# SSM groups of a two-block network on one core: the gate product in a PSUM bank of its own, and five scalings moved from VectorE to ScalarE

## The chip, the core and the metric

The kernel runs on one core of one Trainium2 chip. The metric is device time in microseconds of one execution. The engines that matter are TensorE (PE in the rows; PEld is its weight load), VectorE (DVE), ScalarE (ACT), GpSimd (POOL) and SyncE (SP, which issues nearly all the loads). Each works through its own queue in order, and waits for the others on semaphores.

## What is computed

Two network blocks follow each other, each of two layers, on a sequence of 256 rows of 1024 columns in float32. The change lies in the second layer of the second block, in its state-space (SSM) mixer. Cut to that, the reference is:

```
z, xbc, dt = split(u @ w_in)                      # u: 256 x 1024
xs, B, C   = split(silu(conv3(xbc) + bias))       # 8 groups of 4 heads of 64, state 128
dt         = softplus(dt + dt_bias)               # forward and backward
y_f, _ = ssd_chunked(xs, dt[fwd], A[0], B, C, h0_fwd)      # chunks of 128
y_b, _ = ssd_chunked(flip(xs), flip(dt[bwd]), A[1], flip(B), flip(C), h0_bwd)
y = y_f + flip(y_b) + D_skip * xs
y = rmsnorm_per_group(y * silu(z)) * norm_g       # 8 groups of 256 columns
out = y @ w_out
```

and inside a chunk of `ssd_chunked`, for each head: a diagonal part (C B^T times a decay matrix, times dt x), a part from the state at the chunk's start, and the state handed to the next chunk, `h1 = decay * h0 + (decayed B)^T x`.

## The kernel before, in words

Float32 products are made of three products in the chip's replicated float32: every operand is split in a high part (a rounded copy) and a low part (the rest). For weights `Weights` (line 50 on) does this as they arrive: ScalarE casts the high half `wh` (L57), VectorE subtracts to get the low half `wl` (L58), in parts of 512 columns; each of the two has five buffers. `mm3` and `up` (L181) multiply hi by hi, hi by lo, lo by hi.

The SSM mixer (`ssm`, line 1742 on) works through eight groups. For each, `proj` makes four tiles of x, B and C (`xbc`: 24 matmuls each into `ps_xbc`, then a convolution by ScalarE and VectorE, L1548 to L1554) and the gate `z` (48 matmuls in two halves of 24, one for each 128 rows, into `ps_z`), whose silu is `z_sz` (tanh on ScalarE, L1737, and a product on VectorE, L1738). A group needs twelve parts of weights: eight for the four tiles, four for the gate.

`group(g)` (line 1798 on) takes the projections of group g:
- transposes of x, B (`ps_xt`, `ps_bt`) and the product C B^T (`ps_cb`); ScalarE copies x (`z_xt`), B (`z_Bt`) and C B^T (`z_CB`); VectorE makes the weighted x (`z_xw`, L1666) and starts y with the skip, `y = D * x` (L1666, `z_y<-ps_xt`);
- the state of the second chunk: product `ps_h` (L1833), decay of the old one on VectorE (L1666, `z_h<-z_h,z_ediag`), their sum (L1836);
- the decay matrices G: outer sums in PSUM (`ps_r`, L1841, L1842), sixteen exponentials of 128 columns on ScalarE (L1846), the two directions added and multiplied by CB (L1848, L1849), one half of the rows on VectorE, the other on GpSimd;
- for each 128 rows: the part from the states (`ps_off`, scaled by VectorE, L1666, summed by GpSimd, L1858 and L1859) and the diagonal part (`ps_yd`, L1863, added by VectorE, L1864);
- y times the gate on GpSimd (L1865), squares with a sum on ScalarE (`yj`, L1869), an inverse root by eleven small instructions on VectorE (L268 to L273), the norm scaling on VectorE (L1873);
- later, in the middle of the next group, `ends`: y is transposed (`ps_t`, L300), scaled by norm_g on VectorE (`evac_T`, L322), and split in `z_yh` and `yl` (L259, L260).

Group g runs beside the projections of group g + 1; generators put their instructions between the matmuls, and the framework's scheduler sets the order on each queue by priority. PSUM has eight banks: `ps` two (projection tiles and gate in turn), `pa` three (`ps_xt`, `ps_r`, `ps_off`, `ps_yd`, the transposes of y), `pl` two (`ps_bt`, `ps_cb`), `pd` one (`ps_h` in this stage). Since the gate takes its turn in `ps`, the second projection tile after it needs the bank that the gate fills.

Of the kernel before, what the change touches and what calls it, by code (L numbers as in the profile page):

```python
# [8 lines left out]
F32 = mybir.dt.float32  # L9
F32R = mybir.dt.float32r  # L10
I32 = mybir.dt.int32
AF = mybir.ActivationFunctionType
ALU = mybir.AluOpType

P = 128
S = 256
# [48 lines left out]
class Core:  # L65
# [225 lines left out]
    def evac_T(self, src, gcol, bcol, dst, ps=None):  # L291

        nc = self.nc
        hi, lo = dst
        n = src.shape[2] // P
        if n == 8:
            self.spare = self.SPARE
        def trans(pt, t, j):
            for c in range(2):
                nc.tensor.transpose(pt[:, c, t], src[:, t, (j + c) * P:(j + c + 1) * P], self.ident)  # L300
        if ps is None:
            pts = [(self.ps, self.pl)[j // 2 % 2]([P, 2, 2, P], "ps_t") for j in range(0, n, 2)]
            for t in range(2):
                for j in range(0, n, 2):
                    trans(pts[j // 2], t, j)
        for j in range(0, n, 2):
            if ps is None:
                ptj = pts[j // 2]
            else:
                ptj = ps([P, 2, 2, P], "ps_t")  # L310
                for t in range(2):
                    trans(ptj, t, j)

            val = self.t2([P, 2, S], name="ev_t")
            for c in range(2):
                g = gcol[:, j + c:j + c + 1]
                b = 0.0 if bcol is None else bcol[:, j + c:j + c + 1]
                pt = ptj[:, c].rearrange("p t i -> p (t i)")
                if self.EV[j // 2 % 4]:
                    nc.scalar.activation(val[:, c], pt, AF.Identity, bias=b, scale=g)  # L320
                elif bcol is None:
                    nc.vector.tensor_scalar(val[:, c], pt, g, None, op0=ALU.mult)  # L322
                else:
                    nc.vector.tensor_scalar(val[:, c], pt, g, b, op0=ALU.mult, op1=ALU.add)  # L324
            self.split(hi[:, j:j + 2], lo[:, j:j + 2], val)
# [798 lines left out]
class Second(Core):  # L1124
# [600 lines left out]
    def proj(self, g, xp):  # L1725

        nc = self.nc
        w = self.io["ssm_w_in_2"][0]
        tiles = self.xbc(g, (2 * g, 2 * g + 1, 16 + g, 24 + g), xp)
        pz = self.ps([P, 2, S], "ps_z2")  # L1730
        wz = [self.wsplit(w[k * P:(k + 4) * P, g * S:(g + 1) * S].rearrange("(k p) n -> p k n", p=P), 4, S) for k in (0, 4)]
        for t in range(2):
            for k in range(8):
                self.mm3(pz[:, t], tuple(q[:, k, t * P:(t + 1) * P] for q in xp), wz[k // 4].at(k % 4), k == 0, k == 7)
            self.tick()
        sz = self.w2("sz", [P, 2, S], bufs=3)
        nc.scalar.activation(sz, pz, AF.Tanh, scale=0.5)  # L1737
        nc.vector.scalar_tensor_tensor(sz, sz, 1.0, pz, op0=ALU.add, op1=ALU.mult)  # L1738
        return tiles, sz

    def ssm(self, xp):
# [4 lines left out]
        v_, s_, g_ = nc.vector, nc.scalar, nc.gpsimd  # L1746
# [3 lines left out]
        identr = self.w2("identr", [P, P], F32R)  # L1750
        s_.copy(identr, self.ident)
        ng = self.const("normg", [P, 16], self.pool2)
        sel32 = self.const("sel", [P, 64], self.pool2)
        sel = self.w2("selr", [P, 64], F32R)
        s_.copy(sel, sel32)
        Dr = self.w2("Dr", [P, 32])
# [20 lines left out]
        wdiag, ediag = (self.w2(n, [P, 2, 32]) for n in ("wdiag", "ediag"))  # L1777
# [20 lines left out]
        def group(g, proj):  # L1798
            h0 = self.w2("h0", [P, 2, S], bufs=2)
            nc.sync.dma_start(h0.rearrange("p d n -> p (d n)"), self.h0d[g])  # L1800
            (xa, xb, Bc, Cc), sz = proj

            px = self.pa([P, 2, S], "ps_xt")
            for t in range(2):
                for c, src in enumerate((xa, xb)):
                    te.transpose(px[:, t, c * P:(c + 1) * P], src[:, t * P:(t + 1) * P], self.ident)
            xt = self.w2("xt", [P, 2, S], bufs=2)
            y = self.w2("y", [P, 2, S], bufs=2)
            xw = self.w2("xw", [P, 2, S])
            both = lambda z, t: z[:, t].rearrange("p (d r) -> p d r", d=2)[:, :, 4 * g:4 * g + 4]  # L1810
            s_.copy(xt, px)
            self.scale_heads(xw, px, wdiag[:, :, 4 * g:4 * g + 4])
            self.scale_heads(y, px, Dr[:, 4 * g:4 * g + 4])
            pb = self.pl([P, 2, P], "ps_bt")
            for t in range(2):
                te.transpose(pb[:, t], Bc[:, t * P:(t + 1) * P], self.ident)
            Bt = self.w2("Bt", [P, 2, P], bufs=2)
            s_.copy(Bt, pb)
            pcb = self.pl([P, 2, P], "ps_cb")
            for t in range(2):  # L1820
                mm(pcb[:, t], Bc[:, t * P:(t + 1) * P], Cc[:, t * P:(t + 1) * P], start=True, stop=True)
            CB = self.w2("CB", [P, 2, P], bufs=2)
            s_.copy(CB, pcb)
            yield

            G = self.w2("G", [P, 2, 2, 4, P])
            for d in range(2):
                if d:
                    yield

                    ph1 = self.psum.tile([P, 2, S], F32, tag="pd", name="ps_h1", bufs=1)
                    for e in range(2):
                        mm(ph1[:, e], Bt[:, e], xw[:, e], start=True, stop=True)  # L1833
                    h1 = self.w2("h1", [P, 2, S], bufs=2)
                    self.scale_heads(h1, h0, ediag[:, :, 4 * g:4 * g + 4])
                    v_.tensor_tensor(h1, h1, ph1, op=ALU.add)  # L1836
                for hp in range(2):
                    pr = self.pa([P, 2, S], "ps_r")
                    for e in range(2):
                        r = d * 32 + 4 * g + 2 * hp + e  # L1840
                        mm(pr[:, e], sel[:, r:r + 1].to_broadcast([P, P]), cumr, start=(e == 0), stop=False, skip_group_check=True)  # L1841
                    mm(pr, identr, trir[:, d].unsqueeze(1).to_broadcast([P, 4, P]), start=False, stop=True, skip_group_check=True)  # L1842
                    for e in range(2):
                        r = d * 32 + 4 * g + 2 * hp + e
                        for t in range(2):
                            s_.activation(G[:, d, t, 2 * hp + e], pr[:, e, t * P:(t + 1) * P], AF.Exp, bias=ncum[:, t, r:r + 1])  # L1846
            for t, z in enumerate((v_, g_)):
                z.tensor_tensor(G[:, 0, t], G[:, 0, t], G[:, 1, t], op=ALU.add)  # L1848
                z.tensor_tensor(G[:, 0, t], G[:, 0, t], CB[:, t].unsqueeze(1).to_broadcast([P, 4, P]), op=ALU.mult)  # L1849
            for t in range(2):  # L1850
                if t == 0:
                    yield
                po = self.pa([P, 2, S], "ps_off")
                for d in range(2):
                    mm(po[:, d], Cc[:, t * P:(t + 1) * P], (h0 if d == t else h1)[:, d], start=True, stop=True)
                tmp = self.t2([P, 2, S], name="yoff")
                self.scale_heads(tmp, po, both(ecum, t))
                g_.tensor_tensor(tmp[:, 0], tmp[:, 0], tmp[:, 1], op=ALU.add)  # L1858
                g_.tensor_tensor(y[:, t], y[:, t], tmp[:, 0], op=ALU.add)  # L1859
                yield  # L1860
                py = self.pa([P, 4, 64], "ps_yd")
                for h in range(4):
                    mm(py[:, h], G[:, 0, t, h], xt[:, t, h * 64:(h + 1) * 64], start=True, stop=True)  # L1863
                v_.tensor_tensor(y[:, t], py.rearrange("p h i -> p (h i)"), y[:, t], op=ALU.add)  # L1864
            g_.tensor_tensor(y, y, sz, op=ALU.mult)  # L1865
            ss = self.sm(2, "y_ss")
            junk = self.t2([P, 2, S], name="yj")
            for t in range(2):
                s_.activation(junk[:, t], y[:, t], AF.Square, accum_out=ss[:, t:t + 1])  # L1869
            v_.tensor_scalar(ss, ss, 1.0 / (4 * S), 1e-6, op0=ALU.mult, op1=ALU.add)  # L1870
            rs = self.rsqrt(ss, 2)
            for t in range(2):
                v_.tensor_scalar(y[:, t], y[:, t], rs[:, t:t + 1], 0.5, op0=ALU.mult, op1=ALU.mult)  # L1873
            ends.append(lambda: self.evac_T(y, ng[:, 2 * g:2 * g + 2], None, yp(2 * g, 2, slice(None)), self.pa))

        projs, ends = [first], []
# [253 lines left out]
```

## Time and profile before

| what | value |
|---|---|
| median of 3 runs | 2434.46 us (2431.4 to 2436.79) |
| the profiled execution's own time | 2440.55 us |
| its span in the profile | 2438.8 us |
| granted TensorE clock over the span | 0.987 |
| TensorE busy | 2327.1 us (95%) |
| VectorE busy | 1779.1 us (73%) |
| ScalarE busy | 1242.1 us (51%) |
| GpSimd busy | 174.7 us (7%) |

The span runs from the first to the last instruction that the profile shows; the execution's own time holds what lies around it. Busy shares are means over stages of different kinds. In a row of the order of time, the figure in brackets is the idle time of that engine just before the row, with what ended it. Matmuls overlap, so a row of 0.28 us may stand 0.12 us behind the one before it. The SSM groups lie from about 1981 to 2194 us.

### The profile page before, as it was taken

The page shows a single profiled execution, that of the slowest core. Times are in us where ns is not written, and L with a number is a line of the kernel's source. Part 1 is how long each engine was busy: PE and PEld are TensorE (multiplying, and loading weights), DVE is VectorE, ACT ScalarE, POOL GpSimd, SP SyncE. Part 2 cuts the span into 40 slices and gives each one's busy share as a digit, 9 for nine tenths or more (in the row PEclk, how much of TensorE's full clock was granted, in tenths as well). Part 3 has the DMA queues.
Part 4 walks back from the last instruction along what each step waited for, and adds up shares of the span by engine and source line. Part 5 has one row for each costly group of instructions (what it writes and reads, how often), then busy time and mean ns, then how long its engine had stood idle before and what let it go on. Part 6 is the DMA issues. An engine that isn't in the chain of part 4 may idle for free.

```text
span 2438.8 us, 49693 instructions
## 1 busy us (share of the span) xinstructions
PE 2327.1 (95%) x19210; PEld 2048.2 (84%) x19210; DVE 1779.1 (73%) x4082; ACT 1242.1 (51%) x2621; POOL 174.7 (7%) x230
## 2 busy tenths in 40 slices
PE   8899999999999999989999999999999999989998
PEld 6787777799998887778888898888899899877997
DVE  6768976676668868767877655887766789986666
ACT  3334435555555344344455555566555566654554
POOL 0210110000000200200000000000000012330000
PEclk9999999999999999999999999999999999999999
DMA  8645555555667654465556566523566644437664
GB/s 243 204 142 153 169 150 116 139 175 168 185 189 216 178 165 129 140 192 164 158 166 170 148 185 206 143 70 96 173 187 183 177 132 129 121 109 225 197 183 130
DMA packets 511277, 396.56 MB, mean 163 GB/s; under 512 B 49776, under 2 KB 444832, under 8 KB 510784
## 3 DMA queue, kind: packets, MB, share of 16 engines
q1 hardware_dynamic: 510096, 391.11, 54.8%
q8 instruction: 151, 2.47, 0.4%
q0 software_dynamic: 944, 2.26, 0.3%
q14 instruction: 86, 0.70, 0.1%
HBM read 386.90 MB, written 6.42 MB: 161 GB/s over the span
## 4 chain that ended last, share of the span: by engine, by line
PE 61%; issue 20%; DVE 11%; ACT 4%; DMA 3%; POOL 1%; SPq 0%; ACTq 0%; DVEq 0%; POOLq 0%
PE ps_fg L181 13%; PE ps_acc L181 9%; PE acc L181 5%; PE ps_gl L181 4%; PE ps_up L181 3%; PE ps_z L181 3%; PE ps_xbc L181 3%; DVE wl L58 2%; PE ps_br L181 2%; PE ps_qk L181 2%; PE ps_o L1487 2%; PE ps_ada L1167 1%; PE ps_q L181 1%; PE ps_pt L1479 1%; PE ps_v L181 1%
## 5 line engine op out<-in xcount | busy, mean ns | idle before, releaser
L58 DVE TENSOR_TENSOR wl<-wr,wh 128x512 fp32r<-128x512 f32 (+1 forms) x1212 | 835.5, 697 | 442.7 <-ACT wh L57 434.6
L57 ACT CAST wh<-wr 128x512 fp32r<-128x512 f32 (+1 forms) x1212 | 741.8, 620 | 796.8 <-PE ps_acc L181 158.1
L181 PE MATMUL ps_fg<-xh,wh 128*128 128x256 f32 x672 | 190.2, 283 | 1.1 <-DVE ev_t L324 1.1
L181 PE MATMUL ps_fg<-xl,wh 128*128 128x256 f32 x672 | 190.2, 283 | 0.0
L181 PE MATMUL ps_fg<-xh,wl 128*128 128x256 f32 x672 | 190.2, 283 | 0.0
L181 PE MATMUL ps_acc<-wh,hh 128*128 128x512 f32 x432 | 170.5, 395 | 0.0
L181 PE MATMUL ps_acc<-wl,hh 128*128 128x512 f32 x432 | 170.4, 394 | 0.0
L181 PE MATMUL ps_acc<-wh,hl 128*128 128x512 f32 x432 | 170.2, 394 | 0.0
L181 PE MATMUL ps_up<-xh,wl 128*128 128x256 f32 x480 | 136.0, 283 | 0.0
L181 PE MATMUL ps_up<-xl,wh 128*128 128x256 f32 x480 | 136.0, 283 | 0.0
L181 PE MATMUL ps_up<-xh,wh 128*128 128x256 f32 x480 | 135.9, 283 | 0.0
L181 PEld LDWEIGHTS ps_fg<-xh,wh 128*128 128x128 f32 x672 | 129.0, 192 | 1.7 <-ACT wh L57 1.2
L181 PEld LDWEIGHTS ps_fg<-xl,wh 128*128 128x128 f32 x672 | 129.0, 192 | 0.4
L181 PEld LDWEIGHTS ps_fg<-xh,wl 128*128 128x128 f32 x672 | 129.0, 192 | 0.0
L181 PE MATMUL ps_fg<-ch,wh 128*128 128x256 f32 x352 | 101.8, 289 | 0.0
L181 PE MATMUL ps_gl<-xh,wh 128*128 128x256 f32 x336 | 98.9, 294 | 1.9 <-ACT th L975 1.5
L181 PE MATMUL ps_fg<-ch,wl 128*128 128x256 f32 x352 | 100.6, 286 | 0.0
L181 PE MATMUL ps_fg<-cl,wh 128*128 128x256 f32 x352 | 100.0, 284 | 0.0
L181 PE MATMUL ps_gl<-xl,wh 128*128 128x256 f32 x336 | 98.5, 293 | 0.0
L181 PEld LDWEIGHTS ps_acc<-wh,hl 128*128 128x128 f32 x432 | 81.3, 188 | 19.1 <-DVE hl L260 0.2
L181 PEld LDWEIGHTS ps_acc<-wh,hh 128*128 128x128 f32 x432 | 81.5, 189 | 17.9 <-ACT hh L259 0.3
L181 PE MATMUL ps_gl<-xh,wl 128*128 128x256 f32 x336 | 96.2, 286 | 0.0
(661 smaller groups left out, 6460.8 us busy)
## 6 DMA issues: line engine op xcount, KB each, us to landing
wr<-in_w_in_dram SPq DMA_DIRECT2D x110, 512.0 KB
adw<-in_ada_w_dram SPq DMA_DIRECT2D x96, 512.0 KB
wr<-in_ssm_w_in_dram SPq DMA_DIRECT2D x72, 512.0 KB
wr<-in_ffn_w_gate_dram SPq DMA_DIRECT2D x66, 512.0 KB
wr<-in_ffn_w_up_dram SPq DMA_DIRECT2D x66, 512.0 KB
wr<-in_ffn_w_down_dram SPq DMA_DIRECT2D x66, 512.0 KB
wr<-in_w_up_dram SPq DMA_DIRECT2D x64, 512.0 KB
wr<-in_w_down_dram SPq DMA_DIRECT2D x64, 512.0 KB
```

The source lines that it names most:

```text
L57: nc.scalar.copy(hi, raw[:, i:i + self.n])
L58: nc.vector.tensor_tensor(lo, raw[:, i:i + self.n], hi.bitcast(F32), op=ALU.subtract)
L181: mm = lambda *z, **k: self.nc.tensor.matmul(*z, skip_group_check=opened, **k)
L1167: nc.tensor.matmul(pm[32 * g:32 * g + 32], self.csc[:, k], w[:, g * 256:(g + 1) * 256], start=(k == 0), stop=(k == 7))
L1479: nc.tensor.transpose(pt[:, kb], sc[e][c][:, kb * P:(kb + 1) * P], self.ident)
L1487: mm(po[HS[e], c, t], kvs[kb // 2][1][:, kb % 2, g * 64:(g + 1) * 64], ats[e][:, kb], start=(kb == 0), stop=(kb == nk - 1))
```

## The change

It does six things. The gate's product `ps_z` goes into the bank `pd`, and the state product `ps_h` takes turns in `pl` instead. Five scalings of a group move from VectorE to ScalarE: the skip (one instruction of 512 columns becomes four of 2 x 64, one for each head), the decay of the state (one of 512 becomes eight of 64), the two norm scalings (two of 256), and the two evacuations of y^T with norm_g (two of 256, where `evac_T` has two column blocks). The factor 0.5 that the norm scaling carried is put into norm_g once, by GpSimd.

```diff
@@ evac_T
-                if self.EV[j // 2 % 4]:
+                if n == 2 or self.EV[j // 2 % 4]:
                     nc.scalar.activation(val[:, c], pt, AF.Identity, bias=b, scale=g)
@@ proj
-        pz = self.ps([P, 2, S], "ps_z2")
+        pz = self.psum.tile([P, 2, S], F32, tag="pd", name="ps_z2", bufs=1)
@@ ssm
         ng = self.const("normg", [P, 16], self.pool2)
+        g_.tensor_scalar(ng, ng, 0.5, 1.0, op0=ALU.mult, op1=ALU.mult)
...
-            self.scale_heads(y, px, Dr[:, 4 * g:4 * g + 4])
+            hd = [slice(h * 64, (h + 1) * 64) for h in range(4)]
+            for h in range(4):
+                s_.activation(y[:, :, hd[h]], px[:, :, hd[h]], AF.Copy, scale=Dr[:, 4 * g + h:4 * g + h + 1])
...
-                    ph1 = self.psum.tile([P, 2, S], F32, tag="pd", name="ps_h1", bufs=1)
+                    ph1 = self.pl([P, 2, S], "ps_h1")
...
-                    self.scale_heads(h1, h0, ediag[:, :, 4 * g:4 * g + 4])
+                    for e in range(2):
+                        for h in range(4):
+                            s_.activation(h1[:, e, hd[h]], h0[:, e, hd[h]], AF.Copy, scale=ediag[:, e, 4 * g + h:4 * g + h + 1])
...
-                v_.tensor_scalar(y[:, t], y[:, t], rs[:, t:t + 1], 0.5, op0=ALU.mult, op1=ALU.mult)
+                s_.activation(y[:, t], y[:, t], AF.Copy, scale=rs[:, t:t + 1])
```

The scheduler sets the order of each queue anew. Three places show it, all in groups 4 and 5; line numbers behind the skip are 7 higher in the changed kernel (G's exponentials L1846 are L1853 there, the norm L1873 is L1880, its product with CB L1849 is L1856; the skip is L1818 and the decay L1842).

ScalarE in group 4, from the gate's tanh (`z_sz`) on, before:

```order
L1737 ACTIVATE z_sz<-ps_z_25983 128x512
L57 CAST wh<-wr 128x512 x3
L1548 COPY xp_23988<-ps_xbc 128x256
L1549 ACTIVATE z_xbc<-ps_xbc,c_convw 128x256
L1811 COPY z_xt<-ps_xt 128x512
L1818 COPY z_Bt<-ps_bt 128x256
L1823 COPY z_CB<-ps_cb 128x256
L57 CAST wh<-wr 128x512 x2
L1548 COPY xp_23989<-ps_xbc 128x256
```

ScalarE at the same place, now:

```order
L1738 ACTIVATE z_sz<-ps_z_26024 128x512
L57 CAST wh<-wr 128x512 x2
L1842 ACTIVATE z_h_26626<-z_h_26502,z_ediag 128x64 x3
L57 CAST wh<-wr 128x512
L1548 COPY xp_23988<-ps_xbc 128x256
L1549 ACTIVATE z_xbc<-ps_xbc,c_convw 128x256
L1813 COPY z_xt<-ps_xt 128x512
L1823 COPY z_Bt<-ps_bt 128x256
L1828 COPY z_CB<-ps_cb 128x256
L1818 ACTIVATE z_y<-ps_xt,z_Dr 128x2x64
L1880 ACTIVATE z_y<-z_y,rs_y 128x256 x2
L1818 ACTIVATE z_y<-ps_xt,z_Dr 128x2x64 x3
```

Three decays, four skips and two norm scalings came in ahead of G's exponentials, and the two casts behind `z_CB` left this place.

ScalarE in group 5, from the copy of x to the first exponentials (`z_G`), before:

```order
L1811 COPY z_xt<-ps_xt 128x512
L1818 COPY z_Bt<-ps_bt 128x256
L1823 COPY z_CB<-ps_cb 128x256
L1869 ACTIVATE yj,y_ss<-z_y 128x256 x2
L57 CAST wh<-wr 128x512 x2
L1548 COPY xp_23989<-ps_xbc 128x256
L1549 ACTIVATE z_xbc<-ps_xbc,c_convw 128x256
L1846 ACTIVATE z_G<-ps_r,z_ncum 128x128 x8
```

ScalarE at the same place, now:

```order
L1813 COPY z_xt<-ps_xt 128x512
L1823 COPY z_Bt<-ps_bt 128x256
L1876 ACTIVATE yj,y_ss<-z_y 128x256 x2
L1818 ACTIVATE z_y<-ps_xt,z_Dr 128x2x64 x4
L1828 COPY z_CB<-ps_cb 128x256
L57 CAST wh<-wr 128x512
L1548 COPY xp_23989<-ps_xbc 128x256
L1549 ACTIVATE z_xbc<-ps_xbc,c_convw 128x256
L1853 ACTIVATE z_G<-ps_r,z_ncum 128x128 x5
L1880 ACTIVATE z_y<-z_y,rs_y 128x256 x2
L1853 ACTIVATE z_G<-ps_r,z_ncum 128x128 x3
```

Skips and the copy of CB stand behind the squares (`yj`), the norm scalings among the exponentials, and one cast less ahead of them.

VectorE in group 4, around the product of G with CB, before:

```order
L1551 SCALAR_TENSOR_TENSOR z_xbc<-xp_23990,c_convw,z_xbc 128x256
L1848 TENSOR_TENSOR z_G<-z_G 128x512
L1554 SCALAR_TENSOR_TENSOR z_xbc<-z_cvt,z_xbc 128x256
L1849 TENSOR_TENSOR z_G<-z_G,z_CB 128x512
L58 TENSOR_TENSOR wl<-wr,wh 128x512
L1666 TENSOR_TENSOR yoff<-ps_off,z_ecum 128x512
L1550 SCALAR_TENSOR_TENSOR z_xbc<-xp_23988,c_convw,z_xbc 128x256
L58 TENSOR_TENSOR wl<-wr,wh 128x512
```

VectorE at the same place, now:

```order
L1551 SCALAR_TENSOR_TENSOR z_xbc<-xp_23990,c_convw,z_xbc 128x256
L1855 TENSOR_TENSOR z_G<-z_G 128x512
L1554 SCALAR_TENSOR_TENSOR z_xbc<-z_cvt,z_xbc 128x256
L1856 TENSOR_TENSOR z_G<-z_G,z_CB 128x512
L58 TENSOR_TENSOR wl<-wr,wh 128x512 x2
L1666 TENSOR_TENSOR yoff<-ps_off,z_ecum 128x512
L1550 SCALAR_TENSOR_TENSOR z_xbc<-xp_23988,c_convw,z_xbc 128x256
L58 TENSOR_TENSOR wl<-wr,wh 128x512
```

The rows read much alike, but they are not the same low halves. Counted from the kernel's start, 1023 low halves stand ahead of the product before and 1021 now, and the gate of group 5 needs those up to the 1024th; so the three rows that follow now are the gate's last three, where it was one. In group 2 the same count gives two where it was one, and in group 0 three where it was one.

## Rows read from the trace of the kernel before

**Rows 1.** Busy time by stage, four groups, 2035.98 to 2145.54 us, sum and mean:

```profile
sum 109.56, PE 101.59 PEld 98.05 DVE 99.97 ACT 71.92 POOL 32.81; mean PE 25.40 PEld 24.51 DVE 24.99 ACT 17.98 POOL 8.20
```

**Rows 2.** Waits of TensorE, 1981 to 2194: us in total, times, longest us:

```profile
PE ps_xbc L181 <- DVE z_sz L1738: 6.9, 3, 2.3
PE ps_yd L1863 <- DVE z_G L1849: 3.7, 4, 1.9
PE ps_z L181 <- DVE wl L58: 3.6, 4, 1.0
```

**Rows 3.** TensorE in order of time: start us, us, instruction, count [idle before]:

```profile
2090.76 0.38 PE L181 MATMUL ps_xbc<-xh,wh 128*128 128x256 f32 x1 [2.29 <-DVE z_sz L1738]
...
2106.51 0.39 PE L181 MATMUL ps_z<-wl,xh 128*128 128x256 f32 x1 [1.02 <-DVE wl L58]
...
2107.21 1.00 PE L1863 MATMUL ps_yd<-z_xt,z_G 128*128 128x64 f32 x8
...
2112.28 1.00 PE L1863 MATMUL ps_yd<-z_xt,z_G 128*128 128x64 f32 x8
...
2130.12 1.08 PE L1863 MATMUL ps_yd<-z_xt,z_G 128*128 128x64 f32 x8 [0.66 <-DVE z_G L1849]
...
2135.26 1.00 PE L1863 MATMUL ps_yd<-z_xt,z_G 128*128 128x64 f32 x8
```

**Rows 4.** ScalarE in order of time, groups 4 and 5, 2087 to 2142:

```profile
2087.04 0.42 ACT L1869 ACTIVATE yj<-z_y 128x256 f32<-128x256 f32 x1 [2.73 <-POOL z_y L1865]
...
2093.81 0.62 ACT L57 CAST wh<-wr 128x512 fp32r<-128x512 f32 x1 [0.52 <-PE ps_xbc L181]
...
2095.64 0.42 ACT L1553 ACTIVATE z_cvt<-z_xbc 128x256 f32<-128x256 f32 x1 [0.46 <-DVE z_xbc L1551]
...
2100.04 2.23 ACT L1846 ACTIVATE z_G<-ps_r,z_ncum 128x128 f32<-128x128 f32 x8
...
2116.82 0.42 ACT L1869 ACTIVATE yj<-z_y 128x256 f32<-128x256 f32 x1 [0.95 <-POOL z_y L1865]
...
2123.63 2.18 ACT L1846 ACTIVATE z_G<-ps_r,z_ncum 128x128 f32<-128x128 f32 x8
...
2136.88 0.62 ACT L259 CAST z_yh<-ev_t 128x512 fp32r<-128x512 f32 x1 [2.14 <-DVE ev_t L322]
...
2141.82 0.42 ACT L1869 ACTIVATE yj<-z_y 128x256 f32<-128x256 f32 x1 [2.74 <-POOL z_y L1865]
```

**Rows 5.** VectorE in order of time, 2104 to 2126:

```profile
2104.08 1.78 DVE L1849 TENSOR_TENSOR z_G<-z_G,z_CB 128x512 f32<-128x512 f32 x1
2105.78 0.68 DVE L58 TENSOR_TENSOR wl<-wr,wh 128x512 fp32r<-128x512 f32 x1
...
2106.99 0.47 DVE L1550 SCALAR_TENSOR_TENSOR z_xbc<-xp,c_convw,z_xbc 128x256 f32<-128x256 f32 x1
...
2126.15 0.69 DVE L1848 TENSOR_TENSOR z_G<-z_G 128x512 f32<-128x512 f32 x1
```

**Rows 6.** GpSimd in order of time, the gate's product of group 4:

```profile
2115.49 1.29 POOL L1865 TENSOR_TENSOR z_y<-z_y,z_sz 128x512 f32<-128x512 f32 x1 [2.17 <-DVE z_y L1864]
```

**Rows 7.** VectorE groups, 1981 to 2194: count, busy us, mean ns, idle before:

```profile
L322 DVE TENSOR_SCALAR ev_t<-ps_t,c_normg 128x256 f32<-128x256 f32 x15 | 6.5, 473 | 0.7 <-PE ps_t L300 0.7
L1873 DVE TENSOR_SCALAR z_y<-z_y,rs_y 128x256 f32<-128x256 f32 x16 | 6.4, 442 | 0.4
L1666 DVE TENSOR_TENSOR z_h<-z_h,z_ediag 128x512 f32<-128x512 f32 x8 | 6.0, 752 | 0.0
...
L1666 DVE TENSOR_TENSOR z_y<-ps_xt,z_Dr 128x512 f32<-128x512 f32 x8 | 5.4, 677 | 0.0
```

**Rows 8.** ScalarE groups of the whole span, shapes kept apart:

```profile
L1846 ACT ACTIVATE z_G<-ps_r,z_ncum 128x128 f32<-128x128 f32 x128 | 34.9, 409 | 0.0
...
L320 ACT ACTIVATE ev_t<-ps_t,cm 128x256 f32<-128x256 f32 x28 | 14.6, 564 | 9.2 <-PE ps_t L300 8.9 <-DVE cl L260 0.3
...
L1755 ACT CAST z_selr<-c_sel 128x64 fp32r<-128x64 f32 x1 | 0.2, 233 | 0.0
```

## The prediction

> **What bounds the kernel now.** I read the stage table first, then the list of waits, then the queues in order of time. The change touches only the eight SSM groups, some 210 us of a 2438.8 us span, so the question is what sets the pace of a group there. Over four groups [rows 1] the mean group lasts 27.4 us; TensorE is busy 25.40 us of it, VectorE 24.99, ScalarE 17.98. TensorE is nearly full and VectorE is the second fullest. The most that can come back is TensorE's idle time, about 2.0 us a group or 16 us in all. The waits [rows 2] say where it lies: three waits of 2.3 us in which a B/C/x tile (ps_xbc) waits until VectorE has finished the gate product z_sz, 3.7 us for the decay matrix G, and 3.6 us for the low halves wl of the gate's weights. The rows in order of time [rows 3] show these alternate. Groups come in pairs of 54.8 us: in an even group (call it A) TensorE does the diagonal product ps_yd only after the first half of the next gate, in an odd one (B) before it. A has the 2.29 us wait at 2090.76 and a 1.02 us wait at 2106.51, B a 0.66 us wait at 2130.12.
>
> The waits are symptoms; the pace is a ring through four engines. Take one pair. ScalarE squares y (yj, 2087.04) once GpSimd has multiplied it by the gate, and works through its queue to the last of sixteen exponentials of G, which end at 2102.27 [rows 4]. VectorE multiplies G by CB (2104.08 to 2105.86) and only then makes the next low half [rows 5]. TensorE goes on to ps_yd (2107.21) and its second one (2112.28, ends 2113.28) [rows 3]. Then VectorE's sum, GpSimd's product (1.29 us) [rows 6], and the next yj at 2116.82. That repeats for B: exponentials end at 2125.81, ps_yd at 2130.12 and 2135.26, yj of the next A at 2141.82 [rows 3, 4]. ScalarE is only 66% busy, but between a yj and the end of G it has almost no gap: in A 15.2 us with two gaps, 0.52 and 0.46 us, in B 9.0 us with none [rows 4]. Its idle time lies elsewhere, between G and the next yj. So the engine that receives the work is a gate of the ring for 24 us of each 54.8.
>
> **The change, part by part.**
>
> *What leaves VectorE* [rows 7]: per group the skip (0.68 us), the state decay (0.75), two norm scalings (0.44 each) and two evacuations (0.47 each), 3.3 us by durations. Instructions overlap by about 0.08 us (the product that starts at 2104.08 ends at 2105.86, the next row starts at 2105.78 [rows 5]), and contended ones inflate the means, so the queue gets some 2.6 us shorter. That is worth something only where VectorE is the late one.
>
> *What ScalarE gets:* four skips of 128 columns, eight decays of 64, two norms and two evacuations of 256. Eight exponentials of 128 columns with a pointer operand take 2.18 us [rows 4], 0.27 each in a row though each lasts 0.41 [rows 8]; I take 0.27 for a skip. A norm or an evacuation has the length of the 0.564 us row [rows 8], 0.42 in a row with the same overlap. No 64-column scaling with a pointer operand is in the trace: below, the 64-column cast of 0.233 us less the overlap of 0.14 gives 0.09; above, the 0.27 of twice the width. I take 0.24, near the upper end because of the pointer. The sum is 1.08 + 1.92 + 0.84 + 0.84 = 4.7 us a group (3.5 to 4.9).
> The Trainium skill (ScalarE: Activation LUTs, What ACT_TABLE_LOAD costs) prices such an instruction at 186 ns, 0.833 ns a column and 93 ns for the pointer operand, with 93 ns of overlap; by it a decay is 0.24 us, an estimate, and the sum stays as it is; no row here has that form.
>
> *Where that lands.* By the order of the change, most decays and both evacuations fall into ScalarE's idle stretch after G and cost nothing: the cast of y^T waited there 2.14 us for VectorE's evacuation anyway [rows 4]. The cover is that idle time; without it they would cost some 2.5 us a group. The four skips and two norms (1.92 us), and three decays in A (0.72), fall between yj and G, on the ring. In A that is +2.6 us; the two gaps vanish (-1.0: one waited for TensorE behind the gate bank, one for VectorE behind norm and skip), and two casts of weights are put behind G (-1.0): **+0.6**. In B: +1.9, and CB's copy moves behind yj (+0.3), one cast fewer (-0.5), less 0.34 of slack, since VectorE adds G only at 2126.15 [rows 5]: **+1.3**.
>
> *The low halves.* In A the casts that were put off make their low halves late. Before, one low half of the gate's four stands behind the G product on VectorE, and ps_yd starts 1.4 us after that product ends (2105.86 to 2107.21) [rows 3, 5]. Now three stand there in groups 4 and 6, and two in group 2. A low half and the offset scaling together take 1.21 (2105.78 to 2106.99), another low half 0.6 each, the convolution step about 0.4 [rows 5]; the last is ready 2.8 us after the product, and the six matmuls on it take 0.7: **+2.0** there, **+1.4** in group 2.
>
> *The handover back.* From the end of the second ps_yd to the next yj passes 3.54 us in B and 5.56 us in A [rows 3, 4], of which GpSimd's product is 1.29 in B [rows 6] and VectorE's sum a fraction; most of the rest is VectorE's backlog. Without evacuations (0.8) and, in A, the decay (0.6), it shrinks: **-1.3** in A; in B TensorE itself comes later to ps_yd, so the backlog has drained, **-1.6**.
>
> *The bank.* The three waits of 2.29 us [rows 2, 3] vanish, but they are not a term by themselves: TensorE comes earlier to the same G and the same low halves and waits there. The state product moves into the pair of banks that ps_bt and ps_cb use; each of these is copied out at a group's start and its bank comes round later in the group at the earliest, so it adds no wait. Halving norm_g is one 16-column instruction on an idle GpSimd, nothing.
>
> *Start and tail.* Group 0 has two low halves more behind its product, +0.8. In the last group the norm leaves VectorE ahead of the G product, but skips and norms delay the exponentials by about as much. There the order puts some matmuls of the output projection more ahead of ps_yd, whose wait was 1.9 us [rows 2]; between none and all of it comes back, I take -1.0.
>
> **Sum.** Pair ending in group 2: 0.6 + 1.3 + 1.4 - 2.9 = +0.4; those ending in 4 and 6: +1.0 each; +0.8, -1.0: **+2.2 us**. The profiled execution took 2440.55 us, 6.1 above the median of 2434.46; against it the change gives 2442.8, and against the median **2436.7 us**. A measurement of this kernel tells apart about 0.2%, 4.9 us, so I forecast no change that can be told.
>
> **Rivals.**
> *Faster: the ring has slack, and VectorE was the gate.* Then TensorE's waits for the gate bank go whole (6.9 us) and the tail's 1.0: 2426.6 us. For it: VectorE is 91% busy, ScalarE 66% [rows 1], and A's gaps on ScalarE were caused by others. Against it: 9 us in B without a gap on ScalarE. Chance 0.30.
> The Trainium skill (Perfetto Trace Analysis, Optimizing Scalar/DVE Operations) says that with VectorE saturated it may make sense to hand work to ScalarE; by that rule this rival holds, and the stage table agrees with its premise.
> *Slower: ScalarE takes over as the bound.* Mechanism: in-order ScalarE between yj and G. Its place is the same, but the handovers don't pay: GpSimd's sum of y, not VectorE's backlog, holds the next yj, and only B's evacuations (0.8 us a pair) come back instead of 2.9. Then +2.2 + 3 x 2.1 = +8.5: 2443.0 us. It decides where less than 2.0 us a pair comes back. For it: GpSimd stands idle 2.17 us before its product [rows 6] while the sum of y is still on VectorE. Chance 0.28.
> The Trainium skill (VectorE: DVE Perf Modes, The TRN2 errata) warns that many small tiles each pay a fixed latency; cutting one 512-column decay into eight does that, and the 64-column cast's 0.233 us beside this width agrees.
> *The change does not do what it says:* the gate's bank is free, but the tile after it stops for its own weights instead. That is part of the forecast and gives the same time.
>
> **The numbers.** Forecast 0.42, faster 0.30, slower 0.28; likeliest 2436.7. Both rivals are too likely to be left out, so the range takes in both with their own bounds: the faster one with half of the waits for low halves beside it (1.8 of 3.6 [rows 2]), the slower one with the decays at their upper price (64 times 0.03, 1.9): 2424.8 to 2444.9. Less than 2 in 10 is left outside.
>
> **What would show it.** Right: no wait of ps_xbc for z_sz; ScalarE near 22.5 us a group; in A the wait of ps_z for wl, or of ps_yd, grows from 1 us to 3 or more; a pair stays at 54 to 56 us. Wrong: pairs of 52 us with ScalarE still idle between yj and G (faster rival), or over 57 us (slower); also decays of 0.35 us in a row, or exponentials that wait for ps_r.

## The result, and the profile after

The changed kernel takes **2451.81 us** (median of 6 runs, 2449.43 to 2454.9) against 2435.26 for the kernel before, measured with it (6 runs). The ratio is 1.007, with a 95% interval from 1.006 to 1.008: 16.5 us slower. The forecast was 2436.7, no change that can be told; the time lies above the upper end of its range, 2444.9.

The profiled execution took 2453.22 us; its span is 2451.5 us (2438.8 before), its mean granted clock 0.983 (0.987). The simplest ruler for the stage is the first and the last transpose of B (ps_bt), one for each group. The tile's view gives it, before and after (median duration in the middle, first and last start behind it):

```profile
L1816 PE MATMUL ps_bt<-c_first,z_xbc x16: 272/272/273, 1981.9 to 2168.5; 128*128 128x128 f32 x16
```

```profile
L1821 PE MATMUL ps_bt<-c_first,z_xbc x16: 272/273/273, 1977.4 to 2182.2; 128*128 128x128 f32 x16
```

That is 186.6 us before and 204.8 after, 18.2 more. The stage began 4.5 us earlier in this execution, for reasons that lie ahead of the change (the last product into ps_up starts at 1521.1 us here and at 1525.8 before; the stage's first starts vary from 1970 to 1982 us over the profiles of this study), and what follows it took 1.0 us less, so the span grew by 12.7.

The stage table, two pairs of groups, each from one long stop of TensorE to the next (it answers to [rows 1]; the column behind POOL is the granted clock):

```profile
2051.29:2110.99 59.70, 53.88 (x391) 50.86 (x391) 44.50 (x92) 44.41 (x130) 16.88 (x14) 0.93 0.39 106
2110.99:2170.21 59.22, 54.31 (x396) 51.86 (x396) 45.44 (x93) 44.40 (x130) 16.89 (x14) 0.95 0.41 116
sum 118.92, PE 108.19 PEld 102.72 DVE 89.94 ACT 88.81 POOL 33.77; mean PE 54.09 PEld 51.36 DVE 44.97 ACT 44.40 POOL 16.89
```

A pair lasts 59.5 us instead of 54.8, beyond the 57 that the prediction named as a sign of the slower rival. ScalarE has 22.2 us of work a group (17.98 before), VectorE 22.5 (24.99): the work moved as forecast. What was not forecast stands in the first column: TensorE is busy 27.05 us a group, 1.65 more than in [rows 1], though it computes the same, and the clock is 0.93 and 0.95.

Waits of TensorE and of ScalarE in the stage, 1975 to 2215 us (answers to [rows 2]: total, times, longest):

```profile
ACT ev_t L320 <- PE ps_t L300: 13.5, 4, 4.4
PE ps_z L181 <- DVE wl L58: 11.7, 5, 3.0
ACT z_h L1842 <- DMA z_h<-h0d: 7.2, 4, 2.8
PE ps_xbc L181 <- DVE wl L58: 2.3, 4, 1.6
PE ps_xbc L181 <- ACT wh L57: 1.9, 2, 1.1
PE ps_yd L1870 <- DVE z_G L1856: 0.8, 2, 0.4
```

The wait for the gate's bank is gone; the wait of the gate for its low halves has grown from 3.6 to 11.7 us. In order of time, TensorE in groups 4 and 5 (answers to [rows 3]):

```profile
2107.64 0.38 PE L181 MATMUL ps_z<-wh,xh 128*128 128x256 f32 x1 [0.37 <-ACT wh L57]
2110.99 0.58 PE L181 MATMUL ps_z<-wl,xh 128*128 128x256 f32 x1 [2.96 <-DVE wl L58]
...
2113.72 0.95 PE L1870 MATMUL ps_yd<-z_xt,z_G 128*128 128x64 f32 x4
2114.43 0.56 PE L181 MATMUL ps_z<-wl,xh 128*128 128x256 f32 x1
...
2115.64 0.95 PE L1870 MATMUL ps_yd<-z_xt,z_G 128*128 128x64 f32 x4
...
2120.83 1.00 PE L1870 MATMUL ps_yd<-z_xt,z_G 128*128 128x64 f32 x8
...
2138.36 1.07 PE L1870 MATMUL ps_yd<-z_xt,z_G 128*128 128x64 f32 x8 [0.35 <-DVE z_G L1856]
...
2143.89 1.00 PE L1870 MATMUL ps_yd<-z_xt,z_G 128*128 128x64 f32 x8
```

The first ps_yd is in two halves here: one (2113.72) stands ahead of the last five gate products (from 2114.43 on), the other (2115.64) behind them. Before, and in group 2 of the changed kernel, all of it stands behind them.

VectorE shows why TensorE stops at 2110.99: the low half it wants comes behind G's product (answers to [rows 5]):

```profile
2108.58 1.75 DVE L1856 TENSOR_TENSOR z_G<-z_G,z_CB 128x512 f32<-128x512 f32 x1
2110.26 1.28 DVE L58 TENSOR_TENSOR wl<-wr,wh 128x512 fp32r<-128x512 f32 x2
```

And the stretches around that stop show the second cost, in the granted clock (us; busy time and count of PE, PEld, DVE, ACT, POOL; clock):

```profile
2104.00:2108.00 4.00, 3.63 (x24) 3.03 (x22) 3.62 (x7) 4.00 (x14) 1.14 (x1) 1.00 0.51 131
...
2110.90:2113.00 2.10, 2.01 (x9) 2.01 (x10) 2.10 (x5) 0.00 (x0) 0.78 (x1) 0.50 0.31 72
2113.00:2115.00 2.00, 2.00 (x12) 2.00 (x10) 2.00 (x3) 0.42 (x1) 1.18 (x2) 0.50 0.69 204
2115.00:2117.00 2.00, 2.00 (x10) 1.94 (x10) 0.78 (x3) 0.00 (x0) 0.00 (x0) 0.54 0.86 242
2117.00:2119.00 2.00, 2.00 (x17) 1.87 (x16) 0.81 (x2) 0.83 (x3) 0.50 (x1) 1.00 0.25 49
```

For some 6 us after the stop TensorE has the lower of its two clock levels (0.50 of the full clock, so 1.2 instead of 2.4 GHz), and does 9 to 12 products in 2 us instead of 17. It is so after each of the three stops of 2.96 us, and for some 3 us after the one of 1.84 us in group 0. Before the change the clock stayed at 1.00 behind each of the three stops of 2.29 us; here behind the one of [rows 3]:

```profile
2090.76:2093.00 2.24, 2.24 (x18) 2.24 (x19) 2.21 (x9) 2.24 (x7) 0.00 (x0) 1.00 0.75 210
```

ScalarE in order of time, groups 4 to 6 (answers to [rows 4]):

```profile
2090.76 0.41 ACT L1876 ACTIVATE yj<-z_y 128x256 f32<-128x256 f32 x1
...
2104.49 2.29 ACT L1853 ACTIVATE z_G<-ps_r,z_ncum 128x128 f32<-128x128 f32 x8
...
2124.15 0.42 ACT L1876 ACTIVATE yj<-z_y 128x256 f32<-128x256 f32 x1 [0.97 <-POOL z_y L1872]
...
2124.96 1.12 ACT L1818 ACTIVATE z_y<-ps_xt,z_Dr 128x128 f32<-128x128 f32 x4
...
2128.80 0.91 ACT L1880 ACTIVATE z_y<-z_y,rs_y 128x256 f32<-128x256 f32 x2
...
2132.42 2.20 ACT L1853 ACTIVATE z_G<-ps_r,z_ncum 128x128 f32<-128x128 f32 x8
...
2148.26 1.31 ACT L1842 ACTIVATE z_h<-z_h,z_ediag 128x64 f32<-128x64 f32 x5 [2.56 <-DMA z_h<-h0d]
...
2149.98 0.41 ACT L1876 ACTIVATE yj<-z_y 128x256 f32<-128x256 f32 x1
```

### The profile page after: what moved, and what is told of

It is laid out like the page before. It is cut to its first block, busy times and chain, and to the rows that moved or that the text cites. A ratio compares the mean times of both kernels' runs of the same rounds, so it can differ in the third digit from the quotient of the medians.

```text
span 2451.5 us, 49714 instructions
## 1 busy us (share of the span) xinstructions
PE 2336.1 (95%) x19210; PEld 2053.3 (84%) x19210; DVE 1762.7 (72%) x4034; ACT 1275.3 (52%) x2749; POOL 177.4 (7%) x231
## 3 DMA queue, kind: packets, MB, share of 16 engines
HBM read 386.90 MB, written 6.42 MB: 160 GB/s over the span
## 4 chain that ended last, share of the span: by engine, by line
PE 57%; issue 20%; DVE 11%; ACT 6%; DMA 4%; POOL 1%; SPq 0%; ACTq 0%; POOLq 0%; DVEq 0%
PE ps_fg L181 13%; PE ps_acc L181 8%; PE acc L181 6%; PE ps_gl L181 3%; PE ps_up L181 3%; DVE wl L58 3%; PE ps_br L181 2%; PE ps_qk L181 2%; PE ps_z L181 2%; PE ps_o L1487 2%; DMA wr<-in_w_in_dram 1%; PE ps_ada L1167 1%; ACT wh L57 1%; PE ps_q L181 1%; PE ps_xbc L181 1%
## 5 line engine op out<-in xcount | busy, mean ns | idle before, releaser
L181 PE MATMUL ps_fg<-xh,wh 128*128 128x256 f32 x672 | 190.2, 283 | 1.1 <-DVE ev_t L324 1.1
L181 PE MATMUL ps_fg<-xl,wh 128*128 128x256 f32 x672 | 190.2, 283 | 0.0
L181 PE MATMUL ps_fg<-xh,wl 128*128 128x256 f32 x672 | 190.2, 283 | 0.0
```

The source lines that it names most:

```text
L181: mm = lambda *z, **k: self.nc.tensor.matmul(*z, skip_group_check=opened, **k)
```

## The experiments

"The stage" is the time from the first to the last ps_bt in the run's profile, as above; each ratio is to the kernel before in the same job. "Clock lost" is the busy time of TensorE in the stage times what was missing of the full clock, summed over stretches of 1 us. The stage is read from one profiled execution of each kernel, the ratio from all its runs. Named by what they keep of the change: B is the banks, S the skip, D the decay, N the norm, E the evacuations. The changed kernel is BSDNE.

| run | what it is | ratio (95%) | stage, us |
|---|---|---|---|
| before | | 1 | 186.6 |
| after | BSDNE | 1.0070 (1.0060 to 1.0080) | 204.8 |
| e1_warm | BSDNE, stops filled | 1.0052 (1.0037 to 1.0066) | 200.5 |
| e2_halves_first | BSDNE, gate's weights earlier | 1.0030 (1.0015 to 1.0045) | 194.2 |
| e3_bank_decay_evac | BDE | 0.9997 (0.9987 to 1.0008) | 186.8 |
| e4_bank | B | 0.9999 (0.9987 to 1.0010) | 190.2 |
| e5_norm_back | BSDE | 1.0032 (1.0019 to 1.0045) | 194.3 |
| e6_skip_back | BDNE | 1.0032 (1.0021 to 1.0043) | 194.3 |
| e7_decay_back | BSNE | 1.0051 (1.0036 to 1.0066) | 199.9 |
| e8_skip_pool | BDE, skip on GpSimd | 1.0040 (1.0025 to 1.0055) | 194.3 |
| e9_exps_first | BSDNE, exponentials earlier | 1.0056 (1.0041 to 1.0071) | 203.0 |
| e10_bde_exps_first | BDE, exponentials earlier | 0.9987 (0.9978 to 0.9997) | 183.1 |
| e11_bde_halves_first | BDE, gate's weights earlier | 0.9999 (0.9987 to 1.0010) | 187.0 |
| e12_bde_both | BDE, both earlier | 0.9988 (0.9978 to 0.9997) | 182.9 |

**What the low clock costs by itself.**

```diff
+                if t == 0 and k == 2 and g in (1, 3, 5, 7):
+                    for _ in range(24):
+                        nc.tensor.matmul(pz[:, 1], xp[0][:, 0, 0:P], wz[0].at(0)[0], start=True, stop=True, skip_group_check=True)
```

> The changed kernel with 24 extra products ahead of the gate's first late low half in groups 0, 2, 4 and 6 (96 in all, into the half of the gate's bank that is not yet begun, where the true product overwrites them); the queues of the other engines stay nearly as they are. Low-halves theory (TensorE stops 2.96 us in groups 2, 4 and 6, 1.84 in group 0, because the low halves stand behind G's product on VectorE, and after it runs at 0.50 of its clock for 4 to 7 us): the stop is filled with work that counts for nothing, the granted clock stays at 1.00 there, each place gives back about 3 us (2 in group 0), and the time falls from 2452 to 2441 to 2445 us although nothing useful comes earlier. Load theory (ScalarE in order is the bound, and TensorE's clock is not what costs): the next group waits for ScalarE anyhow, 2450 to 2454 us; with the extra products on the path, up to 2460.

Measured: 2448.68 us; the clock is at 1.00 through the whole stage:

```profile
2102.00:2105.00 3.00, 2.65 (x23) 2.44 (x21) 3.00 (x3) 2.28 (x5) 2.16 (x2) 1.00 0.00 0
2105.00:2108.00 3.00, 1.69 (x12) 1.49 (x12) 3.00 (x5) 0.00 (x0) 1.25 (x2) 1.00 0.45 109
2108.00:2111.00 3.00, 2.82 (x22) 2.67 (x22) 2.52 (x6) 0.42 (x1) 0.71 (x1) 1.00 0.72 202
```

The extra products also disturb the gate's sums, against the expectation, so only the time of this run is read. The time lies between the two expectations, and the interval of the ratio (to 1.0066) just overlaps that of the changed kernel (from 1.0060), so I go by the trace: work that counts for nothing made the stage shorter, and the clock is a cost of its own. It is smaller than I expected: the stage is 4.3 us shorter, where 10.9 us of clock had been lost in it. In group 4 the first ps_yd is whole again and stands behind the last gate products; the second follows it by 5.07 us (2108.87 to 2113.94) as before the change. But TensorE, at full speed, waits anew for the next low half (1.03 to 1.14 us in each of groups 2, 4 and 6). From the end of G's product to the second ps_yd group 4 takes 9.2 us, where the changed kernel takes 10.5 and the kernel before 6.4. Part of the slow stretch only covered a wait that came next.

**Low halves ahead of G's product.**

```diff
-        wz = [self.wsplit(...) for k in (0, 4)]
+        with self.tc.high_priority(100):
+            wz = [self.wsplit(...) for k in (0, 4)]
```

> The changed kernel, all five scalings on ScalarE, with the split of the gate's weights (high and low halves) given the priority that the convolution's copies have, so that the four low halves of each gate stand ahead of G's product in groups 0, 2, 4 and 6 (976, 1000, 1024, 1048 low halves counted ahead of it, where it was 973, 998, 1021, 1045). Low-halves theory: no stop of 2.96 us, no stretch at half clock behind it, 2434 to 2440 us, about the time of the kernel before. Load theory: ScalarE has the same work, the casts that go forward push the exponentials and G back, and TensorE waits for G instead: 2447 to 2454 us.

Measured: 2442.34 us. The stops for low halves of the gate are gone, the clock lost in the stage falls from 10.9 to 5.0 us, and 10.6 of the 18.2 us come back. The rest does not; TensorE now waits for G:

```profile
PE ps_yd L1871 <- DVE z_G L1857: 10.9, 7, 2.9
PE ps_xbc L181 <- DVE wl L58: 3.1, 4, 2.6
```

Neither theory holds whole. The place of the low halves, with the clock behind it, is over half of the loss. What is left in this run is a later G: with the casts ahead of them the exponentials of groups 2, 4 and 6 end 18.3 us after yj, where the changed kernel has 16.0 to 16.5.

**Which moves are dear.** The first of these undoes skip and norm, the next two undo one of them each, the fourth undoes the decay; their edits are those hunks of the diff left out.

> The gate in a bank of its own, decay and evacuations on ScalarE, skip and norm left on VectorE. The low halves ahead of G's product are as many as before (975, 985, 999, 1009, 1023, ...). Low-halves theory: no long stop, full clock, 2431 to 2438 us. Load theory: ScalarE gets decay and evacuation, some 3.3 of the 5.4 us a group, so about 60% of the 16.5 us: 2443 to 2447 us. If the wait for the old state's load (7.2 us of ScalarE's idle time in the changed kernel) costs by itself: also 2441 or more.

Measured: 2431.96 us, ratio 0.9997. Banks, decay and evacuations together cost nothing and bring nothing, though they are some 60% of what ScalarE got. The load theory by sum of time falls here. ScalarE waits for the load of the old state in this kernel too (3.6 us in 3 waits), at no cost.

> The changed kernel with the norm scaling back on VectorE; skip, decay and evacuations stay on ScalarE. The low halves counted ahead of G's product in groups 0, 2, 4, 6 are 973, 999, 1023, 1047: as before but for group 0. Order theory (the loss is what the low halves behind G's product cost, with the clock that falls after it): about the time of the kernel before, 2434 to 2440 us. Load theory by ScalarE's time (norm is 0.95 of the 5.4 us a group that it was given): an eighteenth to a fifth back, 2447 to 2450 us. Ring theory (only what stands between the squares of y and the exponentials counts; skip 1.1 us, norm 0.9): half back, about 2443 us.

> The changed kernel with the skip back on VectorE; norm, decay and evacuations stay on ScalarE. Low halves ahead of G's product: 975, 999, 1023, 1047 in groups 0, 2, 4, 6, as before, and one fewer in groups 3 and 5. Order theory: 2434 to 2440 us. Load theory (skip 1.1 of 5.4): 2447 to 2449 us. Ring theory: half back, about 2443 us.

Measured: 2441.11 and 2440.75 us. Skip added to BDE costs 7.5 us of the stage, norm added to BDE costs 7.5 as well. ScalarE between the squares and the last exponential of group 4, in BDE and in BSDE:

```profile
2075.46 0.41 ACT L1872 ACTIVATE yj<-z_y 128x256 f32<-128x256 f32 x1
...
2088.45 2.22 ACT L1849 ACTIVATE z_G<-ps_r,z_ncum 128x128 f32<-128x128 f32 x8
```

```profile
2086.35 0.41 ACT L1874 ACTIVATE yj<-z_y 128x256 f32<-128x256 f32 x1
...
2093.21 1.14 ACT L1815 ACTIVATE z_y<-ps_xt,z_Dr 128x128 f32<-128x128 f32 x4 [1.15 <-DVE z_xw L1666]
2095.76 2.20 ACT L1851 ACTIVATE z_G<-ps_r,z_ncum 128x128 f32<-128x128 f32 x8
...
2100.33 2.29 ACT L1851 ACTIVATE z_G<-ps_r,z_ncum 128x128 f32<-128x128 f32 x8
```

15.21 us against 16.27 (before: 15.23, [rows 4]); with the norm in place of the skip, in BDNE, it is 15.99. With the skip's four instructions in that stretch, and ScalarE waiting 1.15 us in order ahead of them, the exponentials end 1.06 us later. Both times lie between the order theory's 2434 to 2440 and the ring theory's 2443, and far from the load theory's. The count of low halves is not all: the wait for the one that stood behind G's product grew to 2.60 to 2.83 us in groups 2, 4 and 6 of BSDE (1.57 to 1.59 in BDE), and the low clock came behind two of them. A later G makes the low half behind it late too.

> The changed kernel with the decay of the state back on VectorE; skip, norm and evacuations stay on ScalarE. Low halves ahead of G's product: 975, 997, 1021, 1045, so three stay behind it in groups 2, 4 and 6. Order theory: the stops and the low clock stay, 2447 to 2453 us. Load theory (the decay is 2.4 of 5.4 us): 2444 us or less. If the wait for the old state's load, 7.2 us on ScalarE, is what costs: 2440 us or less.

Measured: 2445.08 us, within none of the three expectations; three stops of 2.96 us remain. By the stage the decay costs 4.9 us where skip and norm are on ScalarE (the intervals of the two ratios just overlap), and with the evacuations nothing where they are not (e3).

**The bank alone.**

> Only the banks change: the gate's product in a bank of its own, the state product in the pair of ps_bt and ps_cb; the order of the queues is that of the kernel before but for one product. The forecast's step (the three waits of 2.29 us vanish but are no gain by themselves): 2433 to 2437 us, and waits for G or for low halves grow by about as much. Rival (the bank waits were TensorE's true loss): 2427 to 2430 us.

Measured: 2434.82 us, ratio 0.9999. The three waits of 2.29 us for the bank are gone, and the three of 1.0 us for low halves have become three of 2.58 to 2.60, as the forecast said:

```profile
PE ps_z L181 <- DVE wl L58: 8.2, 4, 2.6
```

In the profile the stage is 3.6 us longer, with 6.7 us of clock lost in it where the kernel before lost none; the times of the runs are equal.

**Off both engines.** BDE with the skip as a GpSimd product of z_xt and z_Dr:

> The kernel of bank, decay and evacuations (skip and norm not on ScalarE) with the skip made by GpSimd from ScalarE's copy of x, so on neither VectorE nor ScalarE. If VectorE's queue still sets the pace there: 0.68 us a group less, up to 5 us, 2427 to 2431 us. If GpSimd's instruction slows VectorE beside it (as its products of G do, 1.5 us for a step of 0.43), or the sum of y then comes later: 2433 to 2438 us.

Measured: 2442.47 us, above both expectations. The instruction takes 1.46 us (mean) instead of VectorE's 0.68, and a step of the inverse root on VectorE beside it took 1.00 us where its neighbours take 0.15. In group 4 ScalarE waits 2.61 us for the convolution on VectorE, where it waited 1.02 in BDE, and the exponentials end 16.72 us after yj instead of 15.21; TensorE then waits 2.63 us for the gate's low half in groups 2, 4 and 6. The instruction that left VectorE's list made VectorE's next results later, not earlier; the order there changed as well, and no run parts the two.

**Exponentials earlier**, in the changed kernel and in BDE:

```diff
+                            with self.tc.high_priority(100):
-                            s_.activation(G[:, d, t, 2 * hp + e], ...)
+                                s_.activation(G[:, d, t, 2 * hp + e], ...)
```

> The changed kernel with G's exponentials given the priority that the convolution's copies have, so that ScalarE does them ahead of the norm scalings in the odd groups and ahead of one scaling of the convolution and a tanh in the even ones; the same work on every engine. Ring theory (what stands on ScalarE between the squares of y and the last exponential sets the pace): some 0.9 us in an odd group and 0.6 to 0.9 in an even one come back, 4 to 6 us in all, 2445 to 2448 us. Load theory (the sum of ScalarE's time): nothing, 2450 to 2453 us. If the norm put off makes the transposes of y late: 2453 us or more.

> The kernel of bank, decay and evacuations (skip and norm on VectorE) with the exponentials first on ScalarE. Ring theory: the same 0.5 to 0.9 us a group come back where that kernel had no long stop, 2425 to 2430 us, less than the kernel before. Rival (the convolution's steps put off make the next tiles and their low halves late): 2431 to 2438 us.

Measured: 2449.54 us in the first; its interval overlaps that of the changed kernel. My reading of the order was wrong there: the norm went behind the first eight exponentials but stayed ahead of the last eight, so an odd group's stretch from yj to the last exponential stayed at 10.45 us (10.47 in the changed kernel). It decides nothing. In BDE a tanh that had waited 1.02 us now stands behind the first eight exponentials and waits no more; from yj to the last exponential group 4 takes 14.08 us instead of 15.21, and the waits of the gate for low halves are nearly gone (5.2 us in BDE):

```profile
PE ps_z L181 <- DVE wl L58: 1.7, 4, 0.4
```

2432.14 us, ratio 0.9987 with an interval that ends at 0.9997: a little faster than the kernel before, and than the changed one by far. Pairs last 53.4 us (54.8 in BDE), so what comes off that stretch comes off the pair. The time lies in the rival's 2431 to 2438, not in the 2425 to 2430 of the ring theory: in the last group the squares now stand behind the exponentials and TensorE stops 3.14 us for the transposes of y.

> The kernel of bank, decay and evacuations with the split of the gate's weights put a little forward, so that the one low half that stood behind G's product in groups 0, 2, 4, 6 stands ahead of it (976, 1000, 1024, 1048), and little else moves. In that kernel TensorE waits 1.57 to 1.59 us for it in groups 2, 4 and 6. Low-halves theory: these waits go, 1 to 1.5 us a place less the 0.6 us by which G's product comes later, 2428 to 2431 us. Rival (G's product takes the wait over whole): 2432 to 2435 us.

> The kernel of bank, decay and evacuations with both priorities, exponentials and the gate's split. The two push at each other on ScalarE: one low half is behind G's product again (999, 1023, 1047). If the exponentials are what counts: as with them alone; if the low half counts: as without either, 2431 to 2434 us.

Measured: 2434.5 us (0.9999) and 2432.65 (0.9988). With one low half forward, TensorE waits 1.32 to 1.35 us for G where it waited 1.58 for the low half: the wait changed hands. With both, the stage is as with the exponentials alone (182.9 and 183.1 us); the times expected of the two cases lie too close together to decide.

## Why the prediction was wrong

I compare the ring's stations of the pair of groups 4 and 5, before [rows 3 to 6] and in the rows above; G's product ends at 2110.33 (2108.58 + 1.75) in A and the exponentials at 2106.78 and 2134.62.

| step | before | after | measured | forecast |
|---|---|---|---|---|
| A: yj to last exponential | 15.23 | 16.02 | +0.8 | +0.6 |
| A: exponentials to G's end | 3.59 | 3.55 | 0.0 | 0 |
| A: G's end to second ps_yd (low halves) | 6.42 | 10.50 | **+4.1** | +2.0 |
| A: second ps_yd to next yj | 4.54 | 3.32 | -1.2 | -1.6 |
| B: yj to first ps_yd | 13.30 | 14.21 | +0.9 | +1.3 |
| B: first to second ps_yd | 5.14 | 5.53 | +0.4 | 0 |
| B: second ps_yd to next yj | 6.56 | 6.09 | **-0.5** | -1.3 |
| pair | 54.8 | 59.2 | +4.4 | +1.0 |

The prediction names a handover by the group that it leads into: its 3.54 us "in B" follow the second ps_yd of A (2113.28 to 2116.82), and its 5.56 us "in A" follow that of B. So its -1.6 stands in A's row here, and its -1.3 in B's.

**Right.** The ring through four engines is the pace (in e10 1.1 us off ScalarE's stretch made a pair 1.4 us shorter); the bank's waits are no term by themselves (e4); decays and evacuations together cost nothing (e3), as long as skip and norm stay on VectorE (e7); and three low halves do stand behind G's product and stop TensorE. The prices were good: five decays took 1.31 us, four skips 1.12, two norms 0.91, where I had 0.24, 0.27 and 0.42 each.

**Wrong, first: the low halves, and the clock behind them.** The term for the low halves (+1.4, +2.0 and +2.0 in groups 2, 4 and 6) priced a stop alone, and too low. From the end of G's product to the second ps_yd these groups took 4.7, 4.1 and 4.8 us more (6.4 each before), 13.6 where the sum had 5.4: over half of the 15.6 us by which the groups' 17.8 (below) exceed the forecast's 2.2. In e1, at full clock, it is 2.1, 2.7 and 2.7 more, 7.6 in all. So the wait itself was worth 2.2 more than forecast, and the half clock, which the sum had at nothing, put 6.0 on top; e1 has 4.3 of the stage's 18.2 us back, since its extra products make other groups longer (group 0 by 0.6). I had the rows to ask: at 2180.47 before the change TensorE waits 1.94 us for G, and behind it the clock fell:

```profile
2180.47 1.08 PE L1863 MATMUL ps_yd<-z_xt,z_G 128*128 128x64 f32 x8 [1.94 <-DVE z_G L1849]
```

```profile
2182.00:2185.00 3.00, 3.00 (x15) 2.72 (x14) 2.44 (x5) 0.36 (x1) 1.27 (x2) 0.50 0.58 180
```

**Wrong, second: the handover behind B.** The step "Without evacuations (0.8) and, in A, the decay (0.6), it shrinks: -1.3" gave -0.5 behind group 5 and -0.3 behind group 3 (-1.3, as forecast, behind group 1 alone). What holds y there is GpSimd's sum of the offset, not VectorE's list. It took 2.45 us here and behind group 3, where the same step (the first row) took 0.74 before:

```profile
2136.14 0.74 POOL L1858 TENSOR_TENSOR yoff<-yoff 128x256 f32<-128x256 f32 x1 [2.50 <-DVE yoff L1666]
```

```profile
2144.77 2.45 POOL L1865 TENSOR_TENSOR yoff<-yoff 128x256 f32<-128x256 f32 x1 [3.23 <-DVE yoff L1666]
2147.30 0.74 POOL L1866 TENSOR_TENSOR z_y<-z_y,yoff 128x256 f32<-128x256 f32 x1
```

```profile
2148.07 0.43 DVE L1871 TENSOR_TENSOR z_y<-ps_yd,z_y 128x256 f32<-128x256 f32 x1 [1.44 <-POOL z_y L1866]
```

Why it took so long no run here shows. That GpSimd's sum holds the next yj is the mechanism of the slower rival, behind B alone: behind A the handover paid 1.2 to 1.6 us, near the 1.6 forecast. The rival's 2443.0 was too low as well, since it too left out the clock.

**Wrong, third: start and tail.** From each group's yj to the next (group 0 from ps_bt on), the even groups took 1.1, 4.4, 3.6 and 4.0 us more and the odd ones 1.7, 1.1, 0.8 and 1.1: 17.8 us, 13.1 of them in the even groups. I had +0.8 for group 0 and -1.0 for the last group, which gave +1.1 and +1.1. Group 1 has a stop of 1.64 us of a projection tile for its low half that I had not looked for. Nor had I foreseen ScalarE's own waits in order, for the load of the old state (7.2 us) and for the transposes (13.5 us). The first goes with the decay in e7, worth 4.9 us of the stage together; no run took the second alone away.

The Trainium skill (Perfetto Trace Analysis, Optimizing Scalar/DVE Operations) says that with VectorE saturated it may make sense to hand some work to ScalarE, and VectorE was at 91%. The runs here go with it for decay and evacuations only in that they cost nothing, and against it for skip and norm, 7.5 us each.

Three things stay open: how skip and norm share the low halves' new places between them, since the scheduler sets them anew in every variant; how much the transposes' wait on ScalarE costs by itself; and what the evacuations cost alone, which no run moved by themselves.

## What to carry to other kernels

In these runs a scaling moved to an engine with idle time was free only where it fell into that idle time and the rest of the receiver's order had slack; ask where in the receiver's order it lands, and whether the next stage's first instruction stands behind it. Where TensorE's stop gets longer, price the products behind it at half clock as well, as a chance, from rows behind such stops. And when a move makes the scheduler set the order anew, count what now stands behind the late instruction: here the low halves behind G's product, with the clock, cost 4.1 us in a pair of groups, and the two handovers gave back 1.7.

## What was not expected of the hardware

The same stop does not always bring the low clock. Behind three stops of 2.29 us before the change it stayed at 1.00; behind three of 2.58 to 2.60 in e4 it fell to 0.50 each time; behind one of 2.62 in e5 it did not; in e2 it fell behind one of 1.70, and neither behind another of 1.70 nor behind one of 2.59; and in e7, of three stops of 2.96 us, the first left it at 1.00 and the second did not:

```profile
2047.40:2050.00 2.60, 2.08 (x16) 1.94 (x16) 2.60 (x5) 0.00 (x0) 1.31 (x2) 1.00 0.54 137
...
2105.00:2108.00 3.00, 2.89 (x14) 2.89 (x14) 3.00 (x6) 0.00 (x0) 1.58 (x2) 0.50 0.56 145
```

So from these rows a forecast can give the low clock only a chance.
